# An S5 mixer on one core: the kernel matrix in two rotating steps, transposes and small products moved to other pairs

## The chip, the cores and the metric

The kernel runs on one core of one Trainium2 chip. The metric is device time in microseconds (us) of one execution; less is better. Engine names are those of the profile: PE is TensorE, DVE VectorE, ACT ScalarE, POOL GpSimd, SP the queue that issues most transfers.

## What is computed

One inference step of a two-layer backbone on 1024 sample tokens and 128 context tokens of width 1024. Layer 1 mixes the tokens with an S5 state-space layer, layer 2 with a Fourier transform; a gated convolutional FFN follows each. The change touches only the S5 mixer:

```python
abar = exp(lam * dt); bbar = ((abar - 1) / lam) * bmat      # 64 groups, 64 states, 2 directions
bu = einsum('blgc,gpc->blgp', u, bbar)                      # 16 channels of a group into 64 states
h = associative_scan(h_t = abar * h_(t-1) + bu_t)           # forwards and backwards
y = real(einsum('gcp,blgp->blgc', cmat, h))                 # both directions are added
y = gelu(y + d * h_in); z = y @ w_glu + b_glu; out = z[:, :1024] * sigmoid(z[:, 1024:])
```

## The kernel before, in words

The sequence is cut into frames of 8 steps. Inside a frame the recurrence is a matrix; from frame to frame it is a scan. The 64 groups are 8 blocks of 8 groups, and a block is 4 pairs, numbered 0 to 3. The loop of `run` (L1654) makes one iteration per pair, 32 in all, i = 4b + pr. Each engine works through its own instructions in the order in which the program issues them, and SP its transfers too; what differs between engines is ordered by semaphores alone.

Each iteration i issues, in this order:
- `vmm(i+1)`: 16 PE instructions (L1515) from the inputs `u` and the block's matrices `PT` into the PSUM tile V. `PT[0]` serves pairs 0 and 1, `PT[1]` pairs 2 and 3. There are two V tiles, so it waits until `vout(i-1)` has read the other one.
- in pairs 0, 2 and 3 a part of `make_u`, which normalises the input of a later block (PE L1487, ACT L1491 into `hb`).
- `scan(i)`: one DVE scan in V (L1556). `vin(i+1)`: three DVE instructions (L1537 to L1539) that turn V by the tables `sn` and `cs`, then small ACT copies into its edges (L1541 to L1546), for which the next scan waits. `vout(i)`: two DVE instructions (L1567, L1568). `decay(i+2)` on ACT.
- `wmm(i-1)`: 4 PE instructions with the kernel matrix T (L1578) and 32 with `CA` (L1584), and an ACT copy (L1590).
- then two lists, `fill` and `late`, in which the matrices of coming blocks are made a piece at a time.

What goes into the lists, and where it stands before the change (blocks 1 to 5; block 0 and the last two differ):
- `make_p(b+1)` gives the products `pp` (POOL from block 2 on: L1418, three of L1423 and two of L1429 for each half; pair 0 and pair 1) and the transposes `tr` that make `PT` of them (PE L1437, ACT L1440): `tr[0]` late in pair 1, `tr[1]` late in pair 3.
- `tables(b+1)` makes `sn` and `cs`: `s0` (DVE L1307, L1308) in pair 0; `s1` (DVE L983, L984, ACT L1313) and the sines (ACT L1321) in pair 1, the cosines (ACT L1321) in pair 2.
- `make_ca(b+2)` makes `CA` and `Bb`. Two small sums (POOL L1359, L1360) and `bb[0]` (three POOL instructions, L1386 to L1388), then `ca[:3]`, four POOL instructions of which three have 128x1024 elements (L1368 to L1371), all in pair 2; `bb[1]`, five DVE instructions of 128x128 elements (L1386 to L1388, L1395, L1396), and `ca[3:]`, two POOL instructions of 128x1024 (L1372, L1373), in pair 3. These five are the small factor products. `make_p` reads what they leave.
- `make_t(b+1)` makes the kernel matrix: 64 PE instructions (L1459) into two PSUM tiles, each on 64 rows and 32 columns of the array; six ACT copies (L1469 to L1471); two POOL sums (L1472, L1473); on SP a store to DRAM (L1475) and eight loads that bring it back as T (L1478). All of it is late in pair 2.

In the matrix product `j` counts four groups of 32 columns, `a` two groups of 64 rows; before the change `j` and `a` are the outer loops, so four matmuls that follow each other share one part of the array (L1454 to L1462).

Block 0 takes `powers` as well, some 8.7 us of small DVE instructions that `make_ca(2)` needs, and until pair 2 of block 1 `vmm` carries a piece of the conditioning (PE L1252, ACT L1257) in the same PSUM tile. In the last five iterations `early` starts to load what comes after the mixer.

Of the kernel before, what the change touches and what calls it, by code (L numbers as in the profile page):

```python
# [12 lines left out]
AF = mybir.ActivationFunctionType  # L13
# [19 lines left out]
class Net:  # L33
# [73 lines left out]
    def ada_scale(self, lay, i):  # L107

        a = self.px.tile([128, NB, 2], F32, name=f"A{lay}{i}")
        g = self.gv[:, 2 * i + lay][:, :, None].to_broadcast([128, NB, 2])  # L110
# [156 lines left out]
    def ffn(self, lay, post=None, after=None, first=0, out=None):  # L267
# [99 lines left out]
        def last(js):  # L367
# [4 lines left out]
            sq = self.f_tile("c", [128, NT], name="sq")  # L372
            V, A, G = nc.vector, nc.scalar.activation, nc.gpsimd
            order = (2, 1, 0)
# [13 lines left out]
            def sums(b, ti, p):  # L388
# [6 lines left out]
                if ti == order[-1]:  # L395
                    A(sq[:, cols(b % 3)], x, AF.Square)
                elif b == 0:
                    A(r, x, AF.Square)
                else:
                    t = self.f_tile("t", [128, 384], name="sqt")  # L400
                    A(t, x, AF.Square)
                    nc.gpsimd.tensor_tensor(r, r, t, OP.add)
                if by[ti == order[-1]][b] is G:
                    A(x, x, AF.Copy, scale=self.gv[:, 4, b:b + 1])

# [559 lines left out]
class Ssm:  # L965
# [478 lines left out]
    def make_t(self, b):  # L1444

        nc, sp, E = self.nc, self.sp, self.nc.gpsimd
        CA, Bb = self.CA[b], self.Bb[b]
        T = sp.tile([128, 8, 128], F32, tag="T", bufs=2, name="T")
        kc = self.sg.tile([128, 2, 240], F32, tag="kc", bufs=1, name="kc")
        k0 = self.sg.tile([128, 2, 16], F32, tag="k0", bufs=1, name="k0")  # L1450
        self.T[b] = T

        p = [self.bank("misc", 2) for _ in range(2)]
        for j in range(4):  # L1454
            for a in range(2):
                rows = slice(64 * a, 64 * a + 64)
                for dr in range(2):
                    for ri in range(2):
                        nc.tensor.matmul(p[a][32 * j:32 * j + 32, dr * 128:dr * 128 + 128],  # L1459
                                         lhsT=Bb[rows, ri, 2 * j + dr].rearrange("p a b -> p (a b)"),  # L1460
                                         rhs=CA[rows, ri, 2 * j + dr, 2 * dr:2 * dr + 8].rearrange("p a b -> p (a b)"),
                                         start=ri == 0, stop=ri == 1)  # L1462
        return lambda: self.store_t(b, p, T, kc, k0)

    def store_t(self, b, p, T, kc, k0):
        nc, sp, E = self.nc, self.sp, self.nc.gpsimd
        A = nc.scalar.activation
        for a in range(2):
            A(kc[:, a, 0:128], p[a][:, 128:256], AF.Copy)  # L1469
            A(k0[:, a], p[a][:, 0:16], AF.Copy)  # L1470
            A(kc[:, a, 128:240], p[a][:, 16:128], AF.Copy)  # L1471
        E.tensor_tensor(k0, k0, self.DD[:, b], OP.add)  # L1472
        E.tensor_tensor(kc[:, :, 112:128], kc[:, :, 112:128], k0, OP.add)  # L1473
        o = self.kd.offset + b * 2 * 128 * 240
        nc.sync.dma_start(bass.AP(tensor=self.kd.tensor, offset=o, ap=[[240, 128], [128 * 240, 2], [1, 240]]), kc)  # L1475
        for t in range(8):
            src = bass.AP(tensor=self.kd.tensor, offset=o + (7 - t) * 16, ap=[[240, 16], [32 * 240, 8], [1, 128]])
            nc.sync.dma_start(T[16 * t:16 * t + 16], src)  # L1478
# [125 lines left out]
    def run(self):  # L1604
        self.TB = 2
        for nm in ("tab", "BC", "xb", "CA", "Bb", "Bx", "PT", "T", "U", "vd", "dec", "cd", "ysb"):
            setattr(self, nm, {})
        call = lambda fs: [f() for f in fs]
        rest = slice(16, NG)
        room = {}  # L1610

        def piece(n):
            if n < 2:
                room[0] = self.pp.tile([128, 2, 512], F32, tag="y", bufs=1, name="y")
            self.ada_mm(n, room[0][:, n // 2])
        self.squares()
        self.start()
        self.params()
        piece(0)
        self.ada_load(2)  # L1620
        ca, ends, bb = self.make_ca(0)
        self.make_u(0, self.ada_end)
        call(bb)
        self.loads(1)
        self.load_u(0)
        self.load_x(1)
        pp, tr = self.make_p(0)
        call(pp[0])
        tb = self.tables(0)
        call(tb[:2])  # L1630
        piece(1)
        self.ada_load(3)
        call(tr[0])
        call(pp[1])
        call(ca)
        call(tb[2:])
        self.vmm(0)
        self.decay(0)
        self.vin(0)
        piece(2)  # L1640
        self.ada_load(4)
        call(tr[1])
        self.vmm(1)
        ends()
        self.decay(1)
        self.ada_end()
        self.ada_end()
        ca1, ends1, bb = self.make_ca(1)
        call(bb)
        self.diagonal()  # L1650
        self.make_t(0)()
        self.loads(2)
        n = 32
        for i in range(n + 1):  # L1654
            b, pr = divmod(i, 4)
            n1, n2 = b + 1 < 8, b + 2 < 8
            if 1 < i + 1 < n:
                self.vmm(i + 1)
            if pr == 0 and n1 and b:
                self.make_u(b + 1, parts=(2,))  # L1660
                if n2:
                    self.load_x(b + 2)
            elif pr > 1 and n2:
                self.make_u(b + 2, parts=(pr - 2,))
            if i < n:
                self.scan(i)
            if i + 1 < n:
                self.vin(i + 1)
            if i < n:
                self.vout(i)  # L1670
            if i + 2 < n:
                self.decay(i + 2)
            if i:
                self.wmm(i - 1)
            while self.m_ada:
                self.ada_end()
            if i == n:
                self.store_y(b - 1)
                self.n.want(("g", 1), self.nc.vector)
                break  # L1680
            if i == 27:
                self.made.__exit__(None, None, None)
            fill, late = [], []
            if pr == 0:
                if n1 and b:
                    self.load_u(b + 1)
                if b:
                    self.store_y(b - 1)
                if n1:
                    pp, tr = self.make_p(b + 1)  # L1690
                    fill = list(pp[0])
                    if b:
                        tb = self.tables(b + 1)
                        fill += tb[:1]
                if n1 and b:
                    late = [ends]
                if not b:
                    self.make_u(1)
                    self.load_u(1)
                    self.load_x(2)  # L1700
                    tb = self.tables(1)
                    fill += tb[:2] + ca1
                    second = Later(self.nc.vector)
                    self.phases(second, rest)
                    self.phases16(second, rest)
                    late = tr[0] + tb[2:3] + [lambda: self.powers(rest, [second]), ends1]
            if pr == 1:
                if n1:
                    fill = list(pp[1])
                    late = tr[0] + tb[1:3] if b else tb[3:]  # L1710
                if n2:
                    if b + 3 < 8:
                        self.loads(b + 3)
            if pr == 2:
                if n1:
                    late = [lambda: self.make_t(b + 1)()]
                    if b:
                        late += tb[3:]
                if n2:
                    ca, ends, bb = self.make_ca(b + 2)  # L1720
                    bb[0](self.nc.gpsimd if b else self.nc.vector)
                    fill = ca[:3]
            if i == 7:
                late = [self.last_frame]
            if pr == 3 and n1:
                late += tr[1]
                if n2:
                    bb[1]()
                    fill = ca[3:]
            if i >= 27:  # L1730
                late.append(lambda: self.n.early(i - 27))
            call(fill)
            if i == n - 1:
                self.finals()
            call(late)
# [154 lines left out]
```

## Time and profile before

| | |
|---|---|
| three runs | 2411.99, 2413.01 (median), 2415.6 us |
| the profiled execution | 2410.76 us, span 2408.9 us |
| granted TensorE clock, mean | 0.986 of full speed |
| busy over the span | PE 95%, PE weight loads 92%, DVE 61%, ACT 37%, POOL 30% |
| the mixer loop | 45.8 us (first scan) to 305.5 us (last copy of y) |
| chain that ended last | PE 73%, DVE 17%, issue 4%, DMA 3% |

A timeline row reads: start in us, duration in us, engine, line, operation, output<-inputs, shapes, count; in brackets the idle time before it and what ended it. Instructions of one line that follow each other are merged into one row. The duration of an instruction holds what it waits for inside the engine. A DVE or ACT instruction can start a little before the one ahead of it has ended, so that lengths are best read from start to start.

### The profile page before, as it was taken

The numbers are of one execution on the slowest core, as the hardware profiler recorded it, in microseconds if no ns is written. First come the engines' busy times: TensorE is split into PE (matmuls) and PEld (weight loads), VectorE is DVE, ScalarE is ACT, GpSimd is POOL, SyncE is SP. The second block draws the span as 40 slices with busy tenths as digits, with TensorE's granted clock in tenths as the row PEclk, the third lists the DMA queues.
The fourth block names the chain that finished last, engine by engine and source line by source line (L and its number), as shares of the span: only waits on it lengthen the run. The fifth ranks groups of instructions, "written<-read, shape, count | busy, mean of one in ns | idle before, by whom it ended". The sixth has DMA issues, their size and how long they took to land.

```text
span 2408.9 us, 35526 instructions
## 1 busy us (share of the span) xinstructions
PE 2284.9 (95%) x14658; PEld 2207.7 (92%) x14658; DVE 1469.9 (61%) x2327; ACT 879.4 (37%) x1352; POOL 726.9 (30%) x486
## 2 busy tenths in 40 slices
PE   4788899999999999999999999999999999999996
PEld 4677797879999999999999999999999999999996
DVE  8888868895654556445553664764456455554556
ACT  5566653235232223322232354542223322232234
POOL 6588412363221122211221254521112211221124
PEclk9899999999999999999999999999999999999998
DMA  6443496661111111111110131121011101111112
GB/s 221 121 95 91 114 322 225 216 217 32 49 53 36 36 35 53 45 36 35 44 53 27 53 108 36 48 68 36 27 44 53 44 27 44 44 53 36 36 36 79
DMA packets 94520, 182.31 MB, mean 76 GB/s; under 512 B 16948, under 2 KB 57204, under 8 KB 93336
## 3 DMA queue, kind: packets, MB, share of 16 engines
q1 hardware_dynamic: 90824, 170.67, 22.9%
q0 software_dynamic: 2096, 6.62, 0.8%
q8 instruction: 116, 1.90, 0.3%
q10 hardware_dynamic: 1440, 2.75, 0.3%
q14 instruction: 44, 0.36, 0.0%
HBM read 163.70 MB, written 11.53 MB: 73 GB/s over the span
## 4 chain that ended last, share of the span: by engine, by line
PE 73%; DVE 17%; issue 4%; DMA 3%; ACT 2%; POOL 1%; SPq 1%; DVEq 0%; ACTq 0%; POOLq 0%
PE acc L199 64%; DVE c L308 3%; PE f L199 3%; PE f L839 2%; DVE dh L602 2%; DVE dl L602 2%; DMA w_ada<-w_ada 1%; PE misc L1459 1%; PE f L749 1%; DVE X L363 1%; DMA X<-xT 1%; PE y L1584 1%; DVE V L1538 1%; DVE X L364 1%; DVE V L1539 1%
## 5 line engine op out<-in xcount | busy, mean ns | idle before, releaser
L199 PE MATMUL acc<-h,uh 128*128 128x384 f32 (+1 forms) x4992 | 1014.0, 338 | 0.5 <-ACT ysb L1590 0.5
L199 PEld LDWEIGHTS acc<-h,uh 128*128 128x128 f32 x4992 | 884.2, 188 | 14.2 <-issue 10.9
L183 POOL TENSOR_TENSOR ul<-raw,uh 128x1024 fp32r<-128x1024 f32 x104 | 279.5, 2688 | 1232.1 <-ACT uh L182 1232.1
L199 PE MATMUL acc<-h,ul 128*128 128x384 f32 (+1 forms) x2496 | 571.3, 337 | 0.0
L308 DVE SCALAR_TENSOR_TENSOR c<-t,cw,c 128x896 f32<-128x896 f32 x704 | 347.2, 562 | 202.4 <-ACT c L305 202.4
L199 PEld LDWEIGHTS acc<-h,ul 128*128 128x128 f32 x2496 | 448.3, 189 | 0.0
L182 ACT ACTIVATE uh<-raw 128x1024 fp32r<-128x1024 f32 x108 | 113.7, 1053 | 549.6 <-PE acc L199 495.8
L300 DVE COPY wb<-acc 128x2 f32<-128x2 f32 x88 | 13.9, 158 | 405.8 <-PE acc L199 405.8
L363 DVE SCALAR_TENSOR_TENSOR X<-acc,MOD,X 128x768 f32<-128x768 f32 x168 | 169.8, 1010 | 118.3 <-PE acc L199 118.3
L199 PE MATMUL acc<-gh,dh 128*128 128x384 f32 x960 | 220.8, 337 | 18.4 <-DVE X L365 18.4
L199 PE MATMUL acc<-gl,dh 128*128 128x384 f32 x960 | 218.6, 335 | 0.0
L199 PE MATMUL acc<-gh,dl 128*128 128x384 f32 x960 | 218.3, 335 | 0.0
L199 PEld LDWEIGHTS acc<-gh,dh 128*128 128x128 f32 x960 | 168.8, 188 | 26.9 <-PE acc L199 23.6
L336 ACT ACTIVATE gh<-c 128x1152 fp32r<-128x1152 f32 x44 | 51.4, 1169 | 329.2 <-DVE c L331 290.9
L199 PEld LDWEIGHTS acc<-gh,dl 128*128 128x128 f32 x960 | 171.4, 188 | 0.0
L199 PEld LDWEIGHTS acc<-gl,dh 128*128 128x128 f32 x960 | 171.2, 188 | 0.0
L303 ACT ACTIVATE t<-t,wb 128x1024 f32<-128x1024 f32 x88 | 101.4, 1153 | 152.5 <-DVE t L301 152.5
L183 POOL TENSOR_TENSOR dl<-raw,dh 128x1024 fp32r<-128x1024 f32 x40 | 99.8, 2515 | 165.0 <-ACT dh L182 165.0
L305 ACT ACTIVATE c<-t,cb,cw 128x1152 f32<-128x1152 f32 x88 | 118.9, 1351 | 2.9
L301 DVE TENSOR_TENSOR t<-acc,R 128x1152 f32<-128x1152 f32 x88 | 118.6, 1348 | 0.0
L326 ACT ACTIVATE c<-c 128x1152 f32<-128x1152 f32 x44 | 51.4, 1167 | 152.3 <-DVE c L308 152.3
L602 DVE SCALAR_TENSOR_TENSOR dl<-w_ada,SC,dl 128x1024 f32<-128x1024 f32 x50 | 88.9, 1816 | 0.0
(316 smaller groups left out, 2601.6 us busy)
## 6 DMA issues: line engine op xcount, KB each, us to landing
raw<-w_up SPq DMA_DIRECT2D x88, 512.0 KB, 3.6
w_ada<-w_ada SPq DMA_DIRECT2D x80, 512.0 KB, 4.9
raw<-w_down SPq DMA_DIRECT2D x44, 512.0 KB, 3.6
w_ada<-w_ada SPq DMA_DIRECT2D x8, 1024.0 KB, 5.9
raw<-w_glu SPq DMA_DIRECT2D x16, 512.0 KB, 4.6
u<-hb SPq DMA_DIRECT2D x64, 73.0 KB, 3.7
y_scratch<-ysb SPq DMA_DIRECT2D x8, 584.0 KB, 3.7
xt<-x SPq DMA_DIRECT2D x9, 512.0 KB, 8.1
```

Of the source, the lines that this page charges most:

```text
L182: nc.scalar.activation(hi, raw, AF.Copy)
L183: (E or nc.gpsimd).tensor_tensor(lo, raw, hi.bitcast(F32), OP.subtract)
L199: mm(outs[j], lhsT=w, rhs=r[j], start=first and i == 0, stop=last and i == 2)
L301: nc.vector.tensor_tensor(t.rearrange("p (a b) -> p a b", a=3), p[:, :, :384], self.R.rearrange("p (a b) -> p a b", a=3), OP.mult)
L303: nc.scalar.activation(t[:, :NS], t[:, :NS], AF.Identity, bias=wb[:, 0:1])
L305: nc.scalar.activation(c, t, AF.Identity, bias=cb[:, ui:ui + 1], scale=w(1))
L308: nc.vector.scalar_tensor_tensor(o, a, w(i), o, op0=OP.mult, op1=OP.add)
L326: nc.scalar.activation(c, c, AF.Silu)
L336: nc.scalar.activation(gh, c, AF.Copy)
L363: nc.vector.scalar_tensor_tensor(v, p[:, 0:2, :384], s(0), v, op0=OP.mult, op1=OP.add)
L602: nc.vector.scalar_tensor_tensor(o, i, a, o, op0=OP.mult, op1=OP.add)
L839: nc.tensor.matmul(o, lhsT=l, rhs=x, start=kd not in seen, stop=n == last[kd], skip_group_check=True)
```

## The change

The product for T falls into two functions, one for each group of 64 rows, with `j` as the innermost loop, so that neighbouring matmuls lie in different groups of 32 columns. Each has its own PSUM tile and its three ACT copies. The first stands late in pair 2, ahead of the cosines; the second and `store_t` late in pair 3. `tr[1]` moves from late in pair 3 to late in pair 0 of the block that uses it. The small sums and `bb[0]` on POOL move from pair 2 to pair 1, ahead of `pp[1]`; `bb[1]` on DVE moves from pair 3 to pair 2; `ca` stays in pairs 2 and 3. In block 0 `s0` and `s1` move from pair 0 to pair 1, the cosines and `powers` to pair 2, and all of `make_ca(2)` to pair 3, its products on DVE.

```diff
--- before.py
+++ after.py
@@ -1449,26 +1449,28 @@
         kc = self.sg.tile([128, 2, 240], F32, tag="kc", bufs=1, name="kc")
         k0 = self.sg.tile([128, 2, 16], F32, tag="k0", bufs=1, name="k0")
         self.T[b] = T
-
-        p = [self.bank("misc", 2) for _ in range(2)]
-        for j in range(4):
-            for a in range(2):
+        A = nc.scalar.activation
+
+        def part(a):
+
+            def f():
+                p = self.bank("misc", 2)
                 rows = slice(64 * a, 64 * a + 64)
                 for dr in range(2):
                     for ri in range(2):
-                        nc.tensor.matmul(p[a][32 * j:32 * j + 32, dr * 128:dr * 128 + 128],
-                                         lhsT=Bb[rows, ri, 2 * j + dr].rearrange("p a b -> p (a b)"),
-                                         rhs=CA[rows, ri, 2 * j + dr, 2 * dr:2 * dr + 8].rearrange("p a b -> p (a b)"),
-                                         start=ri == 0, stop=ri == 1)
-        return lambda: self.store_t(b, p, T, kc, k0)
-
-    def store_t(self, b, p, T, kc, k0):
+                        for j in range(4):
+                            nc.tensor.matmul(p[32 * j:32 * j + 32, dr * 128:dr * 128 + 128],
+                                             lhsT=Bb[rows, ri, 2 * j + dr].rearrange("p a b -> p (a b)"),
+                                             rhs=CA[rows, ri, 2 * j + dr, 2 * dr:2 * dr + 8].rearrange("p a b -> p (a b)"),
+                                             start=ri == 0, stop=ri == 1)
+                A(kc[:, a, 0:128], p[:, 128:256], AF.Copy)
+                A(k0[:, a], p[:, 0:16], AF.Copy)
+                A(kc[:, a, 128:240], p[:, 16:128], AF.Copy)
+            return f
+        return [part(0), part(1), lambda: self.store_t(b, T, kc, k0)]
+
+    def store_t(self, b, T, kc, k0):
         nc, sp, E = self.nc, self.sp, self.nc.gpsimd
-        A = nc.scalar.activation
-        for a in range(2):
-            A(kc[:, a, 0:128], p[a][:, 128:256], AF.Copy)
-            A(k0[:, a], p[a][:, 0:16], AF.Copy)
-            A(kc[:, a, 128:240], p[a][:, 16:128], AF.Copy)
         E.tensor_tensor(k0, k0, self.DD[:, b], OP.add)
         E.tensor_tensor(kc[:, :, 112:128], kc[:, :, 112:128], k0, OP.add)
         o = self.kd.offset + b * 2 * 128 * 240
@@ -1648,7 +1650,7 @@
         ca1, ends1, bb = self.make_ca(1)
         call(bb)
         self.diagonal()
-        self.make_t(0)()
+        call(self.make_t(0))
         self.loads(2)
         n = 32
         for i in range(n + 1):
@@ -1682,51 +1684,55 @@
                 self.made.__exit__(None, None, None)
             fill, late = [], []
             if pr == 0:
-                if n1 and b:
-                    self.load_u(b + 1)
                 if b:
+                    late = list(tr[1])
+                    if n1:
+                        self.load_u(b + 1)
+                        late.append(ends)
                     self.store_y(b - 1)
+                else:
+                    self.make_u(1)
+                    self.load_u(1)
+                    self.load_x(2)
                 if n1:
                     pp, tr = self.make_p(b + 1)
                     fill = list(pp[0])
+                    tb = self.tables(b + 1)
                     if b:
-                        tb = self.tables(b + 1)
                         fill += tb[:1]
-                if n1 and b:
-                    late = [ends]
+                    else:
+                        fill += ca1
+                        late = list(tr[0])
+            if pr == 1 and n1:
+                if n2 and b:
+                    ca, ends, bb = self.make_ca(b + 2)
+                    bb[0](self.nc.gpsimd)
+                fill = pp[1] + tb[:0 if b else 1]
+                late = (tr[0] if b else [ends1]) + tb[1:3]
+                if b + 3 < 8:
+                    self.loads(b + 3)
+            if pr == 2 and n1:
+                mt = self.make_t(b + 1)
+                late = mt[:1] + tb[3:]
                 if not b:
-                    self.make_u(1)
-                    self.load_u(1)
-                    self.load_x(2)
-                    tb = self.tables(1)
-                    fill += tb[:2] + ca1
                     second = Later(self.nc.vector)
                     self.phases(second, rest)
                     self.phases16(second, rest)
-                    late = tr[0] + tb[2:3] + [lambda: self.powers(rest, [second]), ends1]
-            if pr == 1:
-                if n1:
-                    fill = list(pp[1])
-                    late = tr[0] + tb[1:3] if b else tb[3:]
-                if n2:
-                    if b + 3 < 8:
-                        self.loads(b + 3)
-            if pr == 2:
-                if n1:
-                    late = [lambda: self.make_t(b + 1)()]
-                    if b:
-                        late += tb[3:]
-                if n2:
-                    ca, ends, bb = self.make_ca(b + 2)
-                    bb[0](self.nc.gpsimd if b else self.nc.vector)
+                    self.powers(rest, [second])
+                elif n2:
+                    bb[1]()
                     fill = ca[:3]
+            if pr == 3 and n1:
+                if b and n2:
+                    fill = ca[3:]
+                elif not b:
+                    ca, ends, bb = self.make_ca(2)
+                    bb[0](self.nc.vector)
+                    bb[1]()
+                    fill = ca
+                late = mt[1:]
             if i == 7:
-                late = [self.last_frame]
-            if pr == 3 and n1:
-                late += tr[1]
-                if n2:
-                    bb[1]()
-                    fill = ca[3:]
+                late.append(self.last_frame)
             if i >= 27:
                 late.append(lambda: self.n.early(i - 27))
             call(fill)
```

## Rows read from the trace of the kernel before

**Rows 1.** Busy time by stretches (us, then each engine), block 3 and block 6.
```profile
166.20:196.50 30.30, 26.15 (x309) 23.13 (x308) 26.27 (x34) 18.94 (x61) 26.62 (x24) 0.94 0.39 89
...
257.30:283.40 26.10, 21.84 (x278) 19.27 (x276) 23.77 (x30) 15.83 (x54) 11.38 (x11) 1.00 0.25 72
```

**Rows 2.** Timeline of DVE, from a scan of pair 2 to the next block's.
```profile
180.41 1.38 DVE L1556 TENSOR_TENSOR_SCAN V<-dec,V 128x592 f32<-128x592 f32 x1
...
185.71 1.40 DVE L1556 TENSOR_TENSOR_SCAN V<-dec,V 128x592 f32<-128x592 f32 x1 [0.31 <-ACT V L1546]
190.08 0.77 DVE L1537 TENSOR_TENSOR B<-V,sn 128x584 f32<-128x584 f32 x1 [2.98 <-PE V L1515]
191.18 0.78 DVE L1538 TENSOR_TENSOR V<-V,cs 128x584 f32<-128x584 f32 x1 [0.33 <-ACT cs L1321]
...
194.02 0.40 DVE L1386 TENSOR_TENSOR Bb<-Bm,beta 128x128 f32<-128x128 f32 x1
...
194.78 1.10 DVE L1388 TENSOR_TENSOR Bb<-Bb,Bx 128x128 f32<-128x128 f32 x1
...
196.40 1.39 DVE L1556 TENSOR_TENSOR_SCAN V<-dec,V 128x592 f32<-128x592 f32 x1
...
201.31 0.88 DVE L1307 COPY w<-W 128x144 f32<-128x144 f32 x1
...
203.98 1.38 DVE L1556 TENSOR_TENSOR_SCAN V<-dec,V 128x592 f32<-128x592 f32 x1
...
208.89 0.62 DVE L983 TENSOR_SCALAR wa<-w 128x896 f32<-128x896 f32 x1
...
210.70 1.38 DVE L1556 TENSOR_TENSOR_SCAN V<-dec,V 128x592 f32<-128x592 f32 x1
```

**Rows 3.** Timeline of PE in block 0: the product for T, a rotating product.
```profile
88.56 4.32 PE L1459 MATMUL misc<-CA,Bb 64*32 64x128 f32 x64
...
93.96 1.08 PE L1252 MATMUL V<-w_ada,SC 128*32 128x128 f32 x32
```

**Rows 4.** Timeline of POOL over the same block as Rows 2.
```profile
177.93 0.41 POOL L1386 TENSOR_TENSOR Bb<-Bm,beta 128x128 f32<-128x128 f32 x1
...
189.35 0.25 POOL L1472 TENSOR_TENSOR k<-k,DD 128x32 f32<-128x32 f32 x1 [2.37 <-ACT k L1470]
...
194.67 1.06 POOL L1423 TENSOR_TENSOR P<-gs,Bb 128x512 f32<-128x512 f32 x1
196.56 2.07 POOL L1423 TENSOR_TENSOR P<-Gt,Bx 128x512 f32<-128x512 f32 x2 [0.83 <-DVE Bx L1396]
...
208.22 0.40 POOL L1386 TENSOR_TENSOR Bb<-Bm,beta 128x128 f32<-128x128 f32 x1
```

**Rows 5.** Timeline before the loop: DVE's small products beside POOL, and alone.
```profile
39.02 1.93 POOL L1372 TENSOR_TENSOR CA<-Qt,Cx 128x1024 f32<-128x1024 f32 x1
39.32 1.78 DVE L1359 TENSOR_TENSOR Cx<-Cm 128x128 f32<-128x128 f32 x1
...
41.02 0.28 DVE L1360 TENSOR_TENSOR Cx<-Cm 128x128 f32<-128x128 f32 x1
41.03 2.49 POOL L1373 TENSOR_TENSOR CA<-CA,CAt 128x1024 f32<-128x1024 f32 x1
41.23 2.44 DVE L1386 TENSOR_TENSOR Bb<-Bm,beta 128x128 f32<-128x128 f32 x1
...
44.53 0.28 DVE L1386 TENSOR_TENSOR Bb<-Bm,beta 128x128 f32<-128x128 f32 x1
```

**Rows 6.** Timeline of SP in block 3: the store for T, its eight loads.
```profile
189.96 0.37 SPq L1475 DMA_DIRECT2D k_scratch<-kc  x1
...
193.30 3.68 SPq L1478 DMA_DIRECT2D T<-k_scratch  x8
```

**Rows 7.** Transfers by line: the eight loads of T (count, KB each, us to landing).
```profile
T<-k_scratch SPq DMA_DIRECT2D x64, 64.0 KB, 2.4
```

**Rows 8.** Timeline of DVE in block 0: a wait of pair 3.
```profile
95.59 0.77 DVE L1537 TENSOR_TENSOR B<-V,sn 128x584 f32<-128x584 f32 x1 [4.60 <-ACT m_ada L1257]
```

## The prediction

> **What bounds the kernel now.** I read the busy time by stretches first, then the timeline of each engine over one block, then what ends each wait. The change lies in the mixer loop; the rest of the span follows its end, so a microsecond there is a microsecond of the kernel. Blocks 2 to 5 repeat one pattern, of which block 3 stands here: in 30.30 us PE is busy 26.15, DVE 26.27 and POOL 26.62 [rows 1]. No engine is full, but three nearly are, so look at what stops each one.
>
> DVE carries the chain: scan, three instructions of `vin`, two of `vout`, next scan. A pair with nothing else takes 4.91 us (203.98 to 208.89), four of them 19.64. Between them stand `s0` (2.67, 201.31 to 203.98), `s1` (1.81, 208.89 to 210.70) and the five small products (2.38, 194.02 to 196.40): 26.50 in all. Three waits remain: 2.98 for `vmm`, which stands behind the product for T on PE, 0.33 for the cosines, 0.31 for ACT's edges. That makes 30.1 of the 30.29 from scan to scan (180.41 to 210.70) [rows 2].
>
> POOL goes from 177.93 to 208.22, the same 30.29, and stops for 2.37 (the ACT copies of the T product) and 0.83 (DVE's last small product): 27.1 us of work [rows 4]. So whatever is taken from DVE's waits, POOL allows no block under 27.1, a gain of at most 3.2.
>
> **What DVE and POOL do to each other** decides this case. A small DVE product takes 0.28 us with POOL idle (44.53). Beside POOL it took 1.78 and 2.44: the one begun at 39.32 ended at 41.10, just after POOL's 39.02 to 40.95, the one begun at 41.23 at 43.67, after POOL's 41.03 to 43.52 [rows 5]. The third of the five took 1.10 because POOL's product at 194.67 ended at 195.73 [rows 2, 4]. `scan`, `vin` and `vout` have one input in PSUM and keep their lengths. So a DVE instruction with both inputs in SBUF waits for POOL's current instruction to end, and POOL's next one mostly goes before DVE's next.
>
> **The change part by part.**
>
> The product for T: 64 PE instructions take 4.32 us, 67.5 ns each; 32 that rotate over the four column groups take 1.08, 33.8 ns each [rows 3]. The new order rotates likewise, so each half costs about 1.08; the bounds are 2.16 (rotation brings nothing) and about 0.5 (twice as good again). The first half fits on PE between `wmm` and the next `vmm`, which waits for `vout` anyway, even at 2.16: the 2.98 goes whatever the value. The same edit moves the cosines forward on ACT by the 3 us it waited for the product, and the products put DVE behind ACT's edges, so 0.33 and 0.31 go too: minus 3.6 a block.
>
> `tr[1]` in pair 0: the same 8 PE instructions and two ACT copies. Next late is `vmm` of pair 2, which now waits for those copies; `s0` stands on DVE meanwhile (2.67 [rows 2]), and I cost it at nothing in blocks 1 to 6. In block 7 there is no `s0`, and the price shows: between 0 and 3 us, I take 1.9.
>
> `store_t` a pair later: POOL's two sums now come after all of `ca`; the SP store, its return and eight loads take from 189.96 to 196.98, the last one lands 2.4 us after its issue [rows 6, 7]. With the two sums (189.35 [rows 4]) T is ready some 10 us after these start. `wmm` of pair 0 waits for it, and `tr[0]` and `vmm` of pair 3 behind it on PE, by my estimate 5 us of PE work: 15. DVE wants that `vmm` after two pairs, `s0`, `s1` and a scan, at about 16. So it is hidden, by 1 us. On SP the loads of `x` and `u` queue behind T's; they move with it by a pair and are wanted in pairs 2 and 3, not before. Cost 0, bounds 0 and 3 a block.
>
> `bb[0]` and the small sums on POOL go ahead of `pp[1]`. Then `s1` no longer meets short POOL instructions but those of `pp[1]`, 1.06 us and longer: two waits, 3.2 in place of 1.8. `s0` meets what it met: 2.7 to 3.0. Plus 1.7.
>
> The five products in pair 2. Count from POOL's sums for T, where POOL stands still in each block until ACT has copied, so that the phase is set anew each time. POOL then streams its 27 to 28 us, of which the last 10.5 or so are five 128x1024 instructions (1.93 to some 2.4 each) [rows 4, 5]. The scan of pair 0 starts about 1.1 us before these sums; from it DVE has three pairs, 14.73, and `s0` and `s1`, 3.0 and 3.2, ahead of the products: it reaches them at about 20, some 2.5 us into the 10.5. Each then waits for one POOL instruction. Four waits and a free fifth make about 9; where two products pass at one boundary, as at 41.02 right after the one that had waited [rows 5], 6.5. I take 8.1, nearer to the one-for-one end, since the waits of block 3 and the other blocks are of that kind. The old place cost 2.38: plus 5.7, bounds 4.1 and 6.6. In exchange POOL's 0.83 goes, which is no gain, as POOL now has time to spare.
>
> A rule read against this: the Trainium skill (SBUF — State Buffer, "SBUF: two separate sides") calls the port pair of DVE and GpSimd an exclusive lock, held for a whole instruction by whoever starts first. By it, strictly, a POOL instruction that queued during a DVE product goes before the next one: no doubles, 9 us, and the total below would be 2435. The row at 41.02 shows one double, so the trace differs there, and by doubles wherever they could fall the total would be 2425.
>
> Block: 30.3 - 3.6 + 1.7 + 5.7 = 34.1; take 34.0, plus 3.6 (bounds 2 to 4.7). Four blocks, 2 to 5: plus 14.4.
>
> Blocks 0 and 1: `powers` only moves. Gained: the waits behind T's product, 4.60 in block 0 [rows 8] and 3.6 as above in block 1. Lost: in block 0 POOL starts `ca(2)` only when `powers` has ended, so two of its big instructions meet DVE's eight small products, 3.5; in block 1 DVE comes that much later to its five, so they meet two fewer, 3; `vin` waits for the conditioning's copy, which now stands behind the sines on ACT, 0.7. Estimates all; minus 8.2 plus 7.2, so minus 1, bounds minus 5 and plus 4. Blocks 6 and 7: no products, but the long `s1`, cosines still late on ACT, and `tr[1]` and T late in block 7 where nothing covers them: 26.10 [rows 1] grows by the 1.7 of `s0` and `s1`, block 7 by the 1.9 above and 0.6 for T, less the little that T's product cost there. Plus 4, bounds 0 and 7.
>
> Sum: 14.4 - 1 + 4 = 17.4 on the profiled 2410.76, which is 2.25 under the median of 2413.01; on the median 2430.
>
> **The rivals.** A: the products pass freely. Place: DVE in pair 2. It decides where they cost less than 4.5 us, the value at which a block is 30.3 again (8.1 less 3.6). At 2.4, with `s1` as before, POOL's 27.1 binds: minus 3.2 in four blocks, minus 5 in block 1, plus 2.5 at the end: about 2398. For it: POOL could come to the big instructions earlier or later than I count, and two products can pass at once. Against: the phase is set anew in each block. Chance 0.22.
> B: two of five pass at each boundary and `s1` stays short: a block of 30 to 31 us, total 2409 to 2417. Chance 0.10.
> C: T is late on top of it. It takes 2 us more on SP than I count; PE then holds `vmm` of pair 3 for some 2 us in five blocks: 2440. Chance 0.06.
> D: the rotation brings nothing. The first half still fits, so no time of its own; it is inside the forecast, chance 0.62.
>
> **How the numbers follow.** The forecast's own range is 2420 to 2440. A's values lie below; to leave out no more than 2 in 10 the range reaches down to 2400, and up to 2441. A measurement here tells 0.2%, 4.8 us, from no change. Slower: forecast and C, 0.68; same: B, 0.10; faster: A, 0.22.
>
> **What would show it.** Right: in blocks 2 to 5 the wait for `vmm` at L1537 is gone, the first four DVE products (L1386 on) take 1 to 2.4 us each and end with a POOL instruction of L1370 to L1373, L984 is longer than 1.23, a block takes 33 to 35 us, POOL waits over 4 us for its sums. Each half of L1459 takes about 1.1. Wrong: the products at 0.3 to 0.4 each, blocks near 27, or a long wait at L1578 for T.

## The result, and the profile after

The changed kernel takes 2427.99 us, median of 4 runs (2426.64 to 2431.24); the kernel before, beside it on the same chip, 2414.27 (2411.99 to 2415.60). The ratio is 1.0060, 95% interval 1.0042 to 1.0077: 13.7 us or 0.6% slower. The forecast was 2430, slower with a chance of 0.68.

The profiled execution has a span of 2424.9 us and took 2426.64, 15.9 more than that of before. Line numbers behind the product for T are two higher now: scan L1558, `vin` L1539 to L1541, `vout` L1569 and L1570, `vmm` L1517, POOL's sums L1474 and L1475; the halves of the product are L1462, the loads of T L1480.

Busy time by stretches, block 3 and then block 6, to be held against [rows 1]:
```profile
167.63:201.53 33.90, 27.04 (x306) 23.17 (x306) 31.53 (x35) 18.94 (x63) 26.68 (x24) 0.85 0.36 85
266.59:293.68 27.09, 24.27 (x296) 20.70 (x296) 23.83 (x29) 17.56 (x58) 11.86 (x13) 0.89 0.27 74
```
POOL's work is what it was (26.7 in a block), DVE's busy time has gone from 26.3 to 31.5 with the same instructions (33 from scan to scan in both; the counts take in those that the ends of a stretch cut), and the granted clock of TensorE from 0.94 to 0.85. DVE is busy longer because its instructions are longer. The timeline of DVE shows which, in block 3 [rows 2], and then in the tail:
```profile
167.63 1.39 DVE L1558 TENSOR_TENSOR_SCAN V<-dec,V 128x592 f32<-128x592 f32 x1
170.03 0.77 DVE L1539 TENSOR_TENSOR B<-V,sn 128x584 f32<-128x584 f32 x1 [1.01 <-PE V L1517]
...
178.29 0.77 DVE L1539 TENSOR_TENSOR B<-V,sn 128x584 f32<-128x584 f32 x1 [0.84 <-PE V L1517]
...
182.94 2.05 DVE L984 TENSOR_TENSOR w<-w,wa 128x896 f32<-128x896 f32 x1
184.91 1.38 DVE L1558 TENSOR_TENSOR_SCAN V<-dec,V 128x592 f32<-128x592 f32 x1
...
189.82 1.83 DVE L1386 TENSOR_TENSOR Bb<-Bm,beta 128x128 f32<-128x128 f32 x1
191.57 2.01 DVE L1387 TENSOR_TENSOR Bx<-Bm,beta 128x128 f32<-128x128 f32 x1
193.62 2.40 DVE L1388 TENSOR_TENSOR Bb<-Bb,Bx 128x128 f32<-128x128 f32 x1
196.12 0.29 DVE L1395 TENSOR_TENSOR Bx<-Bb 128x128 f32<-128x128 f32 x1
196.33 0.29 DVE L1396 SCALAR_TENSOR_TENSOR Bx<-Bb 128x128 f32<-128x128 f32 x1
196.53 1.39 DVE L1558 TENSOR_TENSOR_SCAN V<-dec,V 128x592 f32<-128x592 f32 x1
197.83 0.75 DVE L1539 TENSOR_TENSOR B<-V,sn 128x584 f32<-128x584 f32 x1
...
301.60 0.77 DVE L1539 TENSOR_TENSOR B<-V,sn 128x584 f32<-128x584 f32 x1 [1.49 <-PE V L1517]
...
310.97 0.77 DVE L1539 TENSOR_TENSOR B<-V,sn 128x584 f32<-128x584 f32 x1 [4.35 <-PE V L1517]
```
The wait of 2.98 for `vmm` is gone: after the scan at 196.53 `vin` starts at once. The five products take 6.71 us (189.82 to 196.53) in place of 2.38. The timeline of POOL says why, with [rows 4] to compare; two rows of ACT's stand behind it:
```profile
189.14 2.36 POOL L1371 TENSOR_TENSOR CA<-CAt,CA 128x1024 f32<-128x1024 f32 x1
191.46 1.98 POOL L1372 TENSOR_TENSOR CA<-Qt,Cx 128x1024 f32<-128x1024 f32 x1
193.51 2.36 POOL L1373 TENSOR_TENSOR CA<-CA,CAt 128x1024 f32<-128x1024 f32 x1
202.62 0.25 POOL L1474 TENSOR_TENSOR k<-k,DD 128x32 f32<-128x32 f32 x1 [6.74 <-ACT k L1467]
...
200.31 0.18 ACT L1543 ACTIVATE Fin<-V 128x4 f32<-128x4 f32 x1 [6.00 <-DVE V L1541]
...
202.36 0.18 ACT L1467 ACTIVATE k<-misc 128x16 f32<-128x16 f32 x1
```
POOL's instructions end at 191.50, 193.44 and 195.87, DVE's first three products at 191.65, 193.58 and 196.02: each is let go when POOL's is over. Then POOL stands still for 6.74 us, and the last two take 0.29. POOL waits because ACT's copy of `k` (202.36) stands in ACT's order behind copies of the next `vin`, for which ACT waits 6.00 us, since the products hold `vin` up.

PE pays a second time. Its timeline, from the end of block 3 into block 4, and block 7:
```profile
196.49 1.08 PE L1462 MATMUL misc<-CA,Bb 64*32 64x128 f32 x32
201.66 2.21 PE L1517 MATMUL V<-u,PT 128*64 128x146 f32 x16 [4.10 <-DVE C L1570]
...
210.80 1.45 PE L1517 MATMUL V<-u,PT 128*64 128x146 f32 x16 [0.25 <-ACT PT L1440]
...
303.83 1.31 PE L1580 MATMUL y<-u,T 128*128 128x146 f32 x4 [2.28 <-DMA T<-k_scratch]
305.07 4.27 PE L1586 MATMUL y<-C,CA 64*128 64x146 f32 x32
```
The same `vmm` in the kernel before, block 4:
```profile
201.45 1.22 PE L1515 MATMUL V<-u,PT 128*64 128x146 f32 x16 [1.69 <-DVE C L1568]
```
In the changed kernel PE stands idle for 4.10 us (197.56 to 201.66): the next `vmm` waits for `vout`, which comes on DVE only behind the products, a scan and `vin`. Then this `vmm` takes 2.21 us instead of 1.22: the granted clock is 0.50 from 201.6 to 206 us, its lower level of 1.2 GHz, and 1.00 again from 208 us. In block 3, behind a like pause of 3.89 us, DVE waits 1.01 and 0.84 us for the first two `vmm`. In block 7 `vin` first waits 1.49 us for the `vmm` behind `tr[1]`; then T comes 2.28 us late, `wmm` takes 4.27 us at the lower clock, and `vin` waits 4.35.

The changed kernel's last scan starts at 314.61, 16.04 later than before (298.57), which is the whole difference of the two spans (16.0).

### The profile page after: what moved, and what is told of

Its sections match the earlier page's. It is cut to its first block, busy times and chain, and to the rows that moved or that the text cites. A ratio compares the mean times of both kernels' runs of the same rounds, so it can differ in the third digit from the quotient of the medians.

```text
span 2424.9 us, 35549 instructions
## 1 busy us (share of the span) xinstructions
PE 2285.0 (94%) x14658; PEld 2202.1 (91%) x14658; DVE 1489.3 (61%) x2327; ACT 879.2 (36%) x1352; POOL 726.5 (30%) x486
## 4 chain that ended last, share of the span: by engine, by line
PE 75%; DVE 17%; issue 4%; ACT 1%; DMA 1%; POOL 1%; SPq 0%; DVEq 0%; ACTq 0%; POOLq 0%
PE acc L199 66%; DVE c L308 3%; PE f L199 2%; PE f L839 2%; DVE dh L602 1%; DVE dl L602 1%; PE V L1517 1%; PE f L749 1%; DVE X L363 1%; PE y L1586 1%; DVE X L364 1%; DVE room L951 1%; DVE V L1540 1%; DMA w_ada<-w_ada 1%; DVE B L1539 1%
## 5 line engine op out<-in xcount | busy, mean ns | idle before, releaser
L199 PEld LDWEIGHTS acc<-gh,dh 128*128 128x128 f32 x960 | 168.8, 188 | 27.1 <-PE acc L199 23.6
```

The source lines that it names most:

```text
L199: mm(outs[j], lhsT=w, rhs=r[j], start=first and i == 0, stop=last and i == 2)
```

## The experiments

All times stand beside runs of the kernel before on the same chip. Since the change is inside the mixer, I read two things of each run: the ratio, and where the mixer's scans start (the timeline of DVE). The table gives the lengths of blocks from the first scan of one to the first scan of the next, and of block 7 to its last scan.

| kernel | us | ratio to before, 95% interval | blocks 0+1 | 2 to 5 | 6 | 7 | last scan |
|---|---|---|---|---|---|---|---|
| before | 2414.27 | | 90.2 | 121.3 | 26.1 | 15.2 | 298.6 |
| changed | 2427.99 | 1.0060 (1.0042 to 1.0077) | 89.5 | 131.2 | 27.1 | 20.9 | 314.6 |
| a_products_pair3 | 2415.28 | 1.0000 (0.9989 to 1.0011) | 85.2 | 115.0 | 25.7 | 20.3 | 292.0 |
| b_two_steps | 2413.94 | 0.9993 (0.9983 to 1.0004) | 89.5 | 114.4 | 26.5 | 18.3 | 294.4 |
| b_products_pair2 | 2415.01 | 0.9997 (0.9987 to 1.0007) | 88.4 | 120.9 | 28.2 | 15.2 | 298.4 |
| a_products_pool | 2411.69 | 0.9987 (0.9977 to 0.9997) | 85.5 | 116.8 | 27.9 | 21.6 | 297.7 |
| b_rotation | 2399.89 | 0.9937 (0.9923 to 0.9950) | 82.2 | 114.4 | 25.6 | 15.2 | 283.1 |
| a_store_pair2 | 2411.52 | 0.9980 (0.9970 to 0.9990) | 93.0 | 112.5 | 25.0 | 17.6 | 293.8 |
| a_transposes_pair3 | 2433.94 | 1.0074 (1.0061 to 1.0087) | 88.6 | 136.6 | 28.0 | 19.2 | 318.3 |
| mixed | 2394.97 | 0.9930 (0.9917 to 0.9943) | 80.3 | 114.4 | 24.7 | 16.6 | 281.9 |
| a_no_rotation | 2423.55 | 1.0047 (1.0033 to 1.0061) | 90.1 | 133.8 | 27.3 | 21.2 | 318.3 |

**The products back in pair 3** (a_products_pair3):
```diff
 elif n2:
-    bb[1]()
     fill = ca[:3]
...
 if b and n2:
+    bb[1]()
     fill = ca[3:]
```


> The changed kernel with the five small DVE products alone moved back to pair 3, just ahead of the rest of ca; all else as changed. My theory: in pair 2 they cost 6.7 us a block because each of the first three waits for a POOL instruction of 128x1024, and that is what makes the changed kernel slow. Back in pair 3 POOL is at or past its last big instruction when DVE comes to them: 2 to 3.5 us for the five, a block of blocks 2 to 5 of 28.5 to 30 us instead of 32.8, and a time of 2408 to 2416 us. Rival: the block is long for another reason (the new waits for vmm in pairs 0 and 1, the half clock of TensorE, T a pair later): the products get short, but the gain comes back as a wait for vmm or for the sums, and the time stays over 2421 us.

2415.28 us: the 13.7 us are gone, at the upper end of what my theory allowed. Timelines of POOL and DVE, block 3:
```profile
184.09 2.36 POOL L1373 TENSOR_TENSOR CA<-CA,CAt 128x1024 f32<-128x1024 f32 x1
188.50 0.25 POOL L1474 TENSOR_TENSOR k<-k,DD 128x32 f32<-128x32 f32 x1 [2.04 <-ACT k L1467]
...
186.98 0.28 DVE L1386 TENSOR_TENSOR Bb<-Bm,beta 128x128 f32<-128x128 f32 x1
...
188.10 0.28 DVE L1396 SCALAR_TENSOR_TENSOR Bx<-Bb 128x128 f32<-128x128 f32 x1
```
The same five instructions take 1.33 us (186.98 to 188.31) while POOL stands still, and block 3 takes 28.04.

**The products given to POOL** (a_products_pool):
```diff
...
-    bb[1]()
+    bb[1](self.nc.gpsimd)
```
The lines left out let `bb` take an engine, and write the last product as a sum, with its sign taken up in the sums of `make_p`.

> The changed kernel with the same five small products in pair 2 given to POOL (blocks 1 to 5; the last one as a sum, with the sign taken up in the sums of make_p), so that DVE has no instruction there that waits for POOL. My theory: POOL's work of 27.1 us grows by five instructions of about 0.45 us to 29.3, DVE loses 6.7 us a block: a block of 29.3 to 30.5 us instead of 32.8, bound by POOL, and a time of 2410 to 2418 us. Rival (the block is not long for the products): no change beyond 3 us, or POOL's longer work makes it slower, over 2425 us.

2411.69 us, inside the range. Blocks 2 to 5 add up to 116.8 (29.2 each), but unevenly, 26.3 and 33.0 side by side: DVE now runs ahead of POOL. POOL's sums for T then come late for it, T with them, and `vmm` stands on PE behind the `wmm` that waits for T (timelines of PE and DVE, block 3):
```profile
172.50 1.31 PE L1586 MATMUL y<-u,T 128*128 128x146 f32 x4 [6.94 <-DMA T<-k_scratch]
...
179.94 0.77 DVE L1545 TENSOR_TENSOR B<-V,sn 128x584 f32<-128x584 f32 x1 [6.84 <-PE V L1523]
```
POOL itself stands still nowhere from block 2 to block 5, save once for 0.85 us at the start: it is the bound, as the theory said. These two runs show the products as the cause.

**The products' move alone** (b_products_pair2): in the kernel before, `make_ca` with `bb[0]` goes to pair 1 and `bb[1]` to pair 2, in blocks 1 to 5:
```diff
 if pr == 1 and n2:
+    if b:
+        ca, ends, bb = self.make_ca(b + 2)
+        bb[0](self.nc.gpsimd)
...
 if pr == 2 and n2:
+    if b:
+        bb[1]()
     fill = ca[:3]
```


> The kernel before with the move of the small products alone: the small sums and bb[0] on POOL from pair 2 to the head of pair 1, the five DVE products from pair 3 to pair 2; T's product, transposes and powers as before. My theory: in pair 2 the products meet POOL's instructions and take 5 to 9 us instead of 2.4, and s1 about 1 us more; the wait of 2.98 for vmm is covered by them, so a block goes from 30.3 to 31.5 to 34 us, time 2418 to 2430 us. Rival: the products pass in pair 2 as they do in pair 3 (2.4 us) and cover the wait: a block near 28, time about 2400 us.

2415.01 us, no difference: a miss for my theory, and not its rival either. Timelines of POOL and DVE, block 3:
```profile
183.24 2.35 POOL L1371 TENSOR_TENSOR CA<-CAt,CA 128x1024 f32<-128x1024 f32 x1
189.05 0.25 POOL L1472 TENSOR_TENSOR k<-k,DD 128x32 f32<-128x32 f32 x1 [3.46 <-ACT k L1470]
...
183.92 1.82 DVE L1386 TENSOR_TENSOR Bb<-Bm,beta 128x128 f32<-128x128 f32 x1
185.66 0.28 DVE L1387 TENSOR_TENSOR Bx<-Bm,beta 128x128 f32<-128x128 f32 x1
```
In the kernel before POOL's sums for T stand between the third and the fourth large instruction of `ca`, and POOL waits there 3.46 us for ACT. The first product waits for one POOL instruction, the other four pass in the gap: 2.86 us in all (183.92 to 186.78). The block is as long as before all the same: the wait for `vmm` behind T's product shrinks from 2.98 to 1.61 us, while `s1` in pair 1 grows from 1.81 to 3.51. The move by itself costs nothing. What makes it dear is the second move, that of the sums behind all of `ca`.

**The sums back in pair 2** (a_store_pair2), the products staying there:
```diff
-    late = mt[:1] + tb[3:]
+    late = mt + tb[3:]
...
-    late = mt[1:]
```


> The changed kernel with the second half of the product and the store of T back in pair 2, so that POOL's two sums stand between its third and fourth large instruction of ca again; the five DVE products stay in pair 2. The run with the products' move alone showed them nearly free because POOL stood still for 3.46 us just then. My theory now: it is the two moves together that cost the time. With the sums back POOL stops for 1 to 3.5 us while DVE is at the products, these take 2 to 4.5 us instead of 6.7, a block 29 to 31 us instead of 32.8, and the time is 2408 to 2418 us. Rival (the products cost in pair 2 what they cost, wherever the sums stand): a block over 32 us, time over 2423.

2411.52 us, as expected; blocks 3 to 5 even shorter, 27.7. POOL's stop is short, and it is enough (timelines, block 3):
```profile
187.21 2.36 POOL L1371 TENSOR_TENSOR CA<-CAt,CA 128x1024 f32<-128x1024 f32 x1
190.15 0.25 POOL L1474 TENSOR_TENSOR k<-k,DD 128x32 f32<-128x32 f32 x1 [0.58 <-ACT k L1467]
...
187.89 1.82 DVE L1386 TENSOR_TENSOR Bb<-Bm,beta 128x128 f32<-128x128 f32 x1
189.63 0.28 DVE L1387 TENSOR_TENSOR Bx<-Bm,beta 128x128 f32<-128x128 f32 x1
```
With the next two runs this makes a square. All four have the alternating order; the sums of blocks 2 to 5 are: neither moved 114.4 (b_rotation), only the second half and the sums 114.4 (b_two_steps), only the products 112.5 (a_store_pair2), both 131.2 (changed); in the last two the transposes are moved as well, which a_products_pair3 (115.0, only the sums) shows to be no cause. Only both together cost anything there. (In block 0 the sums' move costs by itself, as b_two_steps shows.)

**The two steps alone** (b_two_steps), in the kernel before with the new `make_t`:
```diff
-    late = [lambda: self.make_t(b + 1)()]
+    mt = self.make_t(b + 1)
+    late = mt[:1]
...
-    late += tr[1]
+    late += mt[1:] + tr[1]
```


> The kernel before with only the product for T in two steps and alternating order (first half in pair 2, second half with the store of T in pair 3); products, transposes and powers stay where they were. My theory: the wait of 2.98 us for vmm at the first vin of a block goes, as do the 0.33 and 0.31 beside it, and nothing is paid but what POOL's 27.1 us of work allows: a block of 27.5 to 28.5 us instead of 30.3 in blocks 2 to 5, and a time of 2396 to 2406 us, under both kernels. Rival: T a pair later, or the copies on ACT, take the place of that wait (wmm waits for T, vmm of pair 3 stands behind it): a block of 30 us and more, time 2410 to 2420.

2413.94 us, a miss: blocks 2 to 5 gain 6.9 us (28.6 each, close to my theory), the time hardly anything (the rival's range). Waits of PE over the mixer:
```profile
PE y L1580 <- DMA T<-k_scratch: 10.5, 4, 4.0
```
T comes late four times, by 1.73 to 3.95 us, each time in one of the blocks 2 to 5; yet these are no longer than in the next run. Against that run blocks 0 and 1 lose 7.3 us, block 6 0.9 and block 7 3.1, and in blocks 0, 1 and 7 PE never waits for T. In block 0 it is the lock of DVE and POOL once more (timelines of POOL and DVE, first here, then in the next run):
```profile
76.92 2.36 POOL L1371 TENSOR_TENSOR CA<-CAt,CA 128x1024 f32<-128x1024 f32 x1
79.24 2.38 POOL L1372 TENSOR_TENSOR CA<-Qt,Cx 128x1024 f32<-128x1024 f32 x1
81.70 2.68 POOL L1373 TENSOR_TENSOR CA<-CA,CAt 128x1024 f32<-128x1024 f32 x1
...
79.76 5.17 DVE L1423 TENSOR_TENSOR P<-Gt,Bx 128x512 f32<-128x512 f32 x2
```
```profile
75.55 2.35 POOL L1371 TENSOR_TENSOR CA<-CAt,CA 128x1024 f32<-128x1024 f32 x1
88.39 0.25 POOL L1474 TENSOR_TENSOR k<-k,DD 128x32 f32<-128x32 f32 x1 [10.48 <-ACT k L1467]
...
78.38 1.28 DVE L1423 TENSOR_TENSOR P<-Gt,Bx 128x512 f32<-128x512 f32 x2
```
With the sums behind all of `ca` POOL goes on where it had stood still, and two products of `make_p` that block 0 leaves to DVE take 5.17 us in place of 1.28. Another 1.4 of the 7.3 arises in pair 0, where the two kernels do not differ yet; the rest is mostly longer waits for the conditioning's copy. In block 7 `vin` waits 3.15 us for a `vmm` that stands on PE behind the second half and `tr[1]` (274.07 to 278.45).

**The new product in the old place** (b_rotation), the kernel before with the new `make_t`: the order alternates, and each half is followed by its own copies:
```diff
-    late = [lambda: self.make_t(b + 1)()]
+    late = self.make_t(b + 1)
```


> The kernel before with the alternating order alone: both halves of the product for T, each with its ACT copies, and the store of T stay in pair 2. My theory: two halves of 1.08 us on PE instead of 4.32, so the wait for vmm at the first vin of a block shrinks from 2.98 to about 1 us, and POOL's stop for its sums shrinks with it; a block of blocks 2 to 5 goes from 30.3 to 27.8 to 28.8 us, and the last scan comes 8 to 14 us earlier. If the rest of the kernel follows the mixer's end one for one, the time is 2401 to 2407 us; if, as in the last four runs, an earlier end is eaten up later (waits for w_ada and half clock at 400 to 520 us), 2409 to 2416. Rival on the chip's side: the order of the column groups brings nothing (4.32 us for both halves together): no change of the block, 30.3 us.

2399.89 us, 0.63% faster than before and a little under the range. The last scan comes 15.5 us earlier, 1.5 more than expected, and the time follows by 15.8. Blocks 2 to 5 give 6.9 of it; blocks 0 and 1 give 8.0, of which 2.4 lie in the first pair, behind the product that is made ahead of the loop. Timelines of PE and DVE, pair 2 of block 3, both halves ahead of `vmm`:
```profile
173.76 1.08 PE L1462 MATMUL misc<-CA,Bb 64*32 64x128 f32 x32
175.40 1.08 PE L1462 MATMUL misc<-CA,Bb 64*32 64x128 f32 x32 [0.56 <-ACT hb L1493]
176.41 1.22 PE L1517 MATMUL V<-u,PT 128*64 128x146 f32 x16
...
180.09 0.77 DVE L1540 TENSOR_TENSOR V<-V,cs 128x584 f32<-128x584 f32 x1 [1.65 <-ACT cs L1321]
```
With 2.16 us on PE instead of 4.32 [rows 3] the wait for `vmm` is gone; 1.65 us for the cosines, which stand on ACT behind the copies, remain. No run has the copies split without the new order.

**Without the alternating order** (a_no_rotation), inside the halves of the changed kernel:
```diff
-for dr in range(2):
-    for ri in range(2):
-        for j in range(4):
+for j in range(4):
+    for dr in range(2):
+        for ri in range(2):
```


> The changed kernel with the two steps kept and only the order of the instructions inside each half put back (column group by column group). The prediction held that the rotation brings no time of its own there, since a half of 2.16 us fits before vmm as well. By that theory: halves of about 2.2 us, blocks 2 to 5 within 0.5 us of the changed kernel's 32.8, time 2425 to 2431 us. Rival: TensorE's added 1.1 us a half is late for vmm in pairs 3 and 0 or delays the copies: 1 to 2 us more a block, 2432 to 2440.

2423.55 us, a little under the range; its ratio's interval overlaps that of the changed kernel. Halves of 2.46 us in place of 1.08, blocks 3 and 4 of 33.88 and 33.90 against 33.90 and 33.86. In its profile, the slowest of its six runs, block 5 is longer (33.9 against 31.2) and the last scan 3.7 us later, which the times do not bear out. So the order, which takes a half from 2.46 to 1.08 us, brings nothing that the times show here: PE stands idle for over 4 us behind the second half.

**The transposes back in pair 3** (a_transposes_pair3):
```diff
-    late = list(tr[1])
...
-    late = mt[1:]
+    late = mt[1:] + tr[1]
```


> The changed kernel with the second transposes and their ACT copies back in pair 3, behind the second half of T's product; all else as changed. Theory that the new waits for vmm in pairs 0 and 1 (0.8 to 1.0 us each) come from tr[1] in pair 0: 1.5 to 2 us less a block and 1 to 2 in block 7, time 2416 to 2421 us. Theory that they come from TensorE's half clock and tr[1] hardly counts, as the prediction had it outside block 7: 0 to 3 us less, time 2424 to 2428.

2433.94 us, over both ranges. In blocks 3 and 4 the move counts for nothing, as predicted (33.87 and 33.89): the wait only changes its place, 9.64 and 7.63 for the first two pairs instead of 8.43 and 8.83. Block 7 is 1.7 shorter, block 6 1.0 longer. The rest is in block 2, whose first two pairs are longer (18.3 against 15.9), and in block 5 (33.9 against 31.2), where the five products meet one POOL instruction each as in blocks 3 and 4, 6.74 us in place of 5.25. What else lengthens these two I haven't settled.

**Both good parts** (mixed): block 0 in the order of before, from block 1 on that of the changed kernel, T's product and sums in pair 2 everywhere. Against b_rotation:
```diff
 if pr == 0:
+    if b > 1:
+        late = list(tr[1])
...
 if pr == 1 and n1:
+    if n2 and b:
+        ca, ends, bb = self.make_ca(b + 2)
+        bb[0](self.nc.gpsimd)
...
 if pr == 2 and n1:
+    if b and n2:
+        bb[1]()
...
 if pr == 3 and n1:
-    late += tr[1]
-    bb[1]()
+    if not b:
+        late += tr[1]
+        bb[1]()
```


> A version meant to beat both kernels: block 0 in the order of the kernel before (powers in pair 0, T and the products where they were), from block 1 on the order of the changed kernel with the second half and the store of T in pair 2; the product for T in alternating order everywhere. From the rows of the runs so far: block 0 as with the alternating order alone (50.1 us), block 1 about 31, blocks 2 to 5 about 27.8, block 6 25.2, block 7 15.2 to 17.5; last scan at 279 to 282 us instead of 283.1. If these parts add, 2394 to 2399 us, the best so far; if what block 0 leaves behind (POOL's phase at the start of block 1) undoes the short blocks, 28.5 us a block as with the order alone and 2399 to 2404.

2394.97 us, ratio 0.9930: inside the first range, faster than both kernels, and not to be told from b_rotation by the intervals. But blocks 2 to 5 add up to 114.4, as the rival had it, not the 111 hoped for (four times 27.8); what the last scan gains, 1.2 us, comes from blocks 0 and 1 (1.9) and 6 (0.8), and block 7 gives 1.4 back.

**The kernel before, a second profile** (before_again):

> The kernel before once more, for a second profile on this chip: how much the end of the mixer and the time from there to the end vary between two executions of one kernel. If the loss behind the mixer in the earlier runs (5 to 7 us in the two whose mixer ended 4 to 7 us earlier) is only scatter, the stretch from the last scan to the end here differs from the 2110.3 us of the first profile by a like amount, 3 to 7 us; if it belongs to an early end, it is 2110 to 2112 again.

Its last scan starts at 298.72, 0.15 us from the first profile, but its span is 2417.6: from there to the end 2118.9 us instead of 2110.3. So a difference of this size arises without an early end of the mixer. Within the mixer the parts scatter more than its end: blocks 0 and 1 take 89.1 and block 6 27.7 here, against 90.2 and 26.1. A difference of 1 to 2 us in one of these columns of the table says little. Granted clock in a stretch behind the mixer (us, PE busy, clock, DMA share, GB/s), first profile, then second:
```profile
400.00:420.00 20.00, 14.91 (x73) 0.91 0.63 228
```
```profile
400.00:420.00 20.00, 14.09 (x61) 0.83 0.64 219
```
In the twelve profiles this last part takes 2110.0 to 2111.5 us five times, 2113.8 once and 2115.6 to 2118.9 six times. The long ones come after late and early ends of the mixer, but more often after early ones: five of the six profiles whose last scan starts before 298 us, two of the other six. Whether an early end adds something of its own these profiles do not settle; the times of b_rotation and of mixed follow their last scans all the same. One profile's time says less about such a change than its last scan does. For eight of the ten changed orders the ratio, taken on 2415 us, follows the last scan within 3 us; a_products_pair3 is some 7 us slower than its last scan says, a_no_rotation some 8 faster, which I leave open.

## Why the prediction was right

**Where the time goes** was right: the lock of DVE and POOL outweighs the wait that the change removes. Step by step:

- T's product: halves of 1.08, the wait of 2.98 gone. As predicted; a_no_rotation, with halves of 2.46, shows no cost in its times, as rival D had it.
- `s1` at 2.98 (181.93 to 184.91) for the 3.2 taken, `s0` at 2.40.
- The five products: taken at 8.1, measured 6.71 in blocks 3 and 4. DVE reaches them 21.1 us after POOL's sums (168.72 to 189.82), not 20, since it waits 1.85 for `vmm`; so three POOL instructions stand in the way, not four. In blocks 2 and 5 two products pass at one boundary, and the five take 6.5 and 5.25 us: the other count of the prediction, 6.5, by which the total was 2425.
- The rule of the Trainium skill (SBUF — State Buffer, "SBUF: two separate sides"), that whoever starts first holds the port pair for its whole instruction, agrees with the three ends within 0.15 us of POOL's ends. Who goes next when both have one queued it does not state; the strict alternation that the prediction read into it (2435) holds in blocks 3 and 4, not in 2 and 5.
- A block was to take 34.0: blocks 3 and 4 take 33.9, by errors that cancel: products 1.4 and `s0` and `s1` together 0.8 shorter, and the two waits for `vmm` at the lower clock, which the prediction did not have, 1.9 longer. That it is the clock is read from the rows; no run takes it away by itself. All four blocks: plus 9.9 in place of 14.4, because blocks 2 and 5 (32.3 and 31.2) are shorter. By its own numbers the block was plus 3.7, not 3.6.
- Its signs hold in blocks 3 and 4, but for one: three products, not four, end with a POOL instruction. In blocks 2 and 5 the block is under the 33 it named, and POOL waits 3.8 us for its sums, not over 4.
- Blocks 0 and 1: minus 0.6 for minus 1.
- Blocks 6 and 7: plus 6.7 for 4. Mis-sized was block 7, 5.7 where 2.5 stood: T is late by 2.28 instead of 0.6, and the lower clock stretches `wmm` and `vmm` behind it. a_transposes_pair3 puts the share of `tr[1]` at 1.7 (1.9 predicted).
- `store_t` a pair later at no cost: T is late by 1.50, 1.41 and 2.28 us in blocks 2, 5 and 7 of the changed kernel (PE's `wmm` at 145.14, 246.06 and 303.83), and only in block 7 does DVE wait for it. So rival C's place was right, its blocks wrong. The other price of the move, POOL running on where it had stood still, is told below the list.

That the total came within 2 us is in part luck: blocks 2 to 5 were taken 4.5 too long, blocks 6 and 7 2.7 too short. And one thing the prediction did not see: it counted the products with POOL's sums already behind all of `ca`, but put the whole price on the products' move and none on the sums'. The square of runs shows that in blocks 2 to 5 neither costs anything alone. It also left unsaid that of the 3.6 a block that it counted as gain, b_rotation keeps 1.7 without any of the moves.

## What to carry to other kernels

Before an instruction of DVE is moved beside POOL's stream, look for the place where POOL stands still, and count what else in the same change moves that place: two moves that each cost nothing in blocks 2 to 5 cost 4 us a block together. Try the smallest part of such a change by itself; here the new order of 64 matmuls, with the copies split to match, was worth 0.63%, and the rearrangement around it, made to the same end, turned it into a loss of 0.6%. When a stage is followed by 2100 us of other work that scatters by 8 us between executions, compare the stage's own end in two profiles as well as the times.

## What the runs showed of the hardware that I had not expected

- A pause of PE of 3.9 to 4.2 us in each of blocks 2 to 5 is followed by a lower granted clock (0.50 from 201.6 to 206 us; the mean of block 3 goes from 0.94 to 0.85), and the sixteen instructions of the next `vmm` take 2.21 us instead of 1.22. What holds DVE up in pair 2 so costs it again in the pairs behind.
- Thirty-two PE instructions in alternating column groups take 1.08 us, column group by column group 2.46 (a_no_rotation), at a granted clock of 1.00 in both; 2.46 is more than half of the 4.32 of [rows 3].
- Two executions of one kernel differ by 8.6 us behind the mixer, with the granted clock at 400 to 420 us at 0.91 and 0.83, while the mixer's last scan repeats to 0.15 us (its parts to 1.6).
